# A bidirectional encoder layer on one core: the pool of constants gets another length, so that the tiles above it start elsewhere

## The chip, the cores and the metric

The kernel runs on one core of a Trainium2 chip, in one launch. The metric is the device time of one execution in microseconds (us). The kernel before was run three times; its time is the median of these. The profile is that of one more execution.

## What is computed

One encoder layer (DEPTH is 1) is applied to two groups of tokens with shared weights: 256 tokens of a prompt and 1,024 of a sample, 1,280 rows of 1,024 float32 values in all.

```python
mod = silu(c) @ w_ada + b_ada                       # shift, scale, gate, twice
h = rmsnorm(x, g_pre_mix) * (1 + scale1) + shift1
proj = h @ w_in                                     # 1024 -> 2592 columns
a = rmsnorm(spatial_gating(u_a, v_a, w_s, b_s, g_vn))
o = rmsnorm(gla(q, k, v, g_fwd) + flip(gla(flipped, g_bwd))) * silu(r)
x = x + gate1 * rmsnorm(concat(a, o) @ w_out, g_post_mix)
h = rmsnorm(x, g_pre_ffn) * (1 + scale2) + shift2
up = conv3(h @ w_up) + b_conv                       # 1024 -> 2 * 2816
x = x + gate2 * rmsnorm((silu(gate) * val) @ w_down, g_post_ffn)
```

## The kernel before

**Products.** Nearly every large product is done in three passes: an operand is split into a rounded high part (ACT, L91) and the rest (POOL or DVE, L92), and high x high, low x high and high x low are summed in PSUM. A matmul has a stationary operand (128 columns, loaded as weights) and a moving one (512 columns, or 256 for the prompt alone). TensorE's instructions run in an order written out by hand; so do those of the other engines up to the first 107 us, and from then on a planner orders ACT, DVE, POOL and the DMA queue SP from its own costs.

**Stages**, in the order of time:
- up to 107 us, L347: modulation, transposes of x into the tiles `h1hi` and `h1lo`, and the columns q, k and the gates. The weights are stationary and h1 moves; 240 matmuls of 512 columns, 120 of 256.
- 107 to 457 us, L338 (`group_mm`): four groups of columns of w_in for 10 tiles of tokens, 24 matmuls each, 960 in all, with h1 stationary and weights moving. In between stand the small matmuls of the gated linear attention (L681, L704, L740, L744), of the spatial gating (L573) and `z` (L632, 256 columns).
- 457 to 595 us, L878, L879, L881 (`mix_mm`): the product with w_out, 48 matmuls for each of 10 tiles of tokens, 480 in all. The stationary tiles `mh` and `ml` come from the pool pm for even tiles of tokens and from the pool mixout for odd ones: `prep_m(t + 1, pm if t % 2 else tx)`.
- 595 to 742 us, L1093: the product with w_up for the prompt, 22 blocks of 48 matmuls of 256 columns, with weights stationary and `hp` moving.
- 742 to 1172 us, L1155 (`prod`): the same for the sample by a seven-product scheme, 22 blocks (f) of seven products of 12 matmuls, 1,848 in all; weights are stationary, the prepared `bop` tiles move.
- 1172 us to the end, L1300: the product with w_down, 1,155 matmuls, then the last norm and the output.

**Where tiles lie.** Each of the 128 partitions of the on-chip memory is filled from both ends: pools with `side="right"` are stacked downwards from the top, the others upwards. The first pool on the left is `const` (`cp`); all other pools of the left side start where it ends. In the compiled program it holds these tiles (bytes per partition, in order; a tile takes a multiple of 32):

```
ident 512, mhalf 4 (takes 32), c1 384, cs 1024, sel 256, AB 128, modT1 128,
modT2 128, gc 128, A2 64, B2d 16 (takes 32), c2 704        = 3520
const starts at 16512 and ends at 20032 = 39 x 512 + 64
the right side's first pool (rp, raw tiles) ends at 229344 = 447 x 512 + 480
```

The operand tiles are multiples of 512 bytes long and are cut at multiples of 512 (128 columns of 4 bytes). So every operand of these products on the left starts at remainder 64 of 512, every one on the right at 480. On the left lie `h1` (h1hi, h1lo), `sg`, `sg2`, `mixout` (mh and ml of odd tiles), `hb` (three of the bop_21 tiles), `h2` (hp), `sf` (two weight slots of the sample's up product, S1 to S4, ug, uv, ag, av) and `dn`. On the right lie the weight slots `wp`, `wx`, `wo` and `wr`, `pm` (mh and ml of even tiles), `bo` (all other bop tiles but the five first ones, which use slots of `wp`), the raw tiles and `dr` (both operands of L1300).

In the sample's up product a counter picks the weight slot (L1124):

```python
def wop(name, src, eng=None):
    if wstate["i"] % 8 < 6:
        w = fslot(f"ws{f}_{name}")                                # pool wr, right
    else:
        w = sf.tile([P, 2, 512], F32R, tag="w", ..., bufs=2)      # left
    wstate["i"] += 1
```

It stands at 42 when this stage begins and is raised seven times in each of the 22 blocks, so 38 of the 154 products have their weights on the left. 402 of their 456 matmuls have a moving operand on the right, and 54 one on the left too. Of the other products, 144 matmuls move a bop_21 tile on the left past weights on the right.

**The gates** (`store_gates`, L803). Once, ahead of the group g = 9, DVE forms the 32 columns `gc` in two halves, TensorE transposes them, DVE copies the result into a raw tile `gate_rows`, and SP stores it. Raw tiles come from a pool of four slots:

```python
def raw_tile(name):
    return rp.tile([P, 512], F32, tag="raw", name=name, bufs=4)
```

The loads of w_in, w_out, w_up and w_down pass through the same four slots.

Of the kernel before, what the change touches and what calls it, by code (L numbers as in the profile page):

```python
# [8 lines left out]
F32 = mybir.dt.float32  # L9
# [8 lines left out]
P = 128  # L18
D = 1024
KT = 8  # L20
# [14 lines left out]
def encoder_kernel(ctx: ExitStack, tc: tile.TileContext, x_prompt, x_sample, c_prompt, c_sample,  # L35
# [6 lines left out]
    def pool(name, bufs=1, side="left", space=None):  # L42
        if space is None:
            cm = tc.tile_pool(name=name, bufs=bufs, side=side, reuse_waits="tile")
        else:
            cm = tc.tile_pool(name=name, bufs=bufs, space=space, reuse_waits="tile") if space == PSUM else tc.tile_pool(name=name, bufs=bufs, space=space)
        p = cm.__enter__()
        return p, lambda: cm.__exit__(None, None, None)
# [15 lines left out]
    cp, cp_close = pool("const")  # L64
# [11 lines left out]
    def gtile(name, shape=(P, 512)):  # L76
        gstate.append(gstate.pop(0))
        return gstate[-1].tile(list(shape), F32, tag="g", name=name)
# [8 lines left out]
    def raw_tile(name):  # L87
        return rp.tile([P, 512], F32, tag="raw", name=name, bufs=4)
# [16 lines left out]
    ident = cp.tile([P, P], F32, name="ident")  # L105
    make_identity(nc, ident)
    mhalf = cp.tile([P, 1], F32, name="mhalf")
    nc.vector.memset(mhalf, -0.5)

    su, su_close = pool("startup", side="right")  # L110
# [43 lines left out]
    def col(name, n):  # L154
        return c1[:, R1[name]:R1[name] + n]
# [644 lines left out]
        nc.vector.tensor_copy(wsT, pt)  # L800

    def store_gates():
        gc = cp.tile([P, 4, KT], F32, name="gc")  # L803
        for i, (gate, gname) in enumerate(((mods[1][:, 0:8, :], "g_post_mix"), (mods[2][:, 8:16, :], "g_post_ffn"))):
            nc.vector.tensor_tensor(out=gc[:, 2 * i:2 * i + 2, :], in0=gate.rearrange("p k s -> p s k"),
                                    in1=col(gname, 8).unsqueeze(1).to_broadcast([P, 2, KT]), op=ALU.mult)
        pt = gtile("pt_gate")
        nc.tensor.transpose(pt[0:32, 0:P], gc.rearrange("p s k -> p (s k)"), ident)
        gr = raw_tile("gate_rows")[0:32, 0:P]
        nc.vector.tensor_copy(gr, pt[0:32, 0:P])  # L810
        for i in range(2):
            nc.sync.dma_start(gate_d[i].rearrange("o (r p) -> (o r) p", p=P), gr[16 * i:16 * i + 16, :])

    for g in range(4 * NT):
# [21 lines left out]
        if g == 9:  # L836
            store_gates()
            load_ws()
# [514 lines left out]
```

## Time and profile before

| | us |
|---|---|
| three runs | 1463.11, 1467.68, 1468.05 |
| median | 1467.68 |
| profiled execution, its own time | 1463.15 |
| its span, first to last instruction | 1461.4 |

In the profile PE is TensorE's matmuls, PEld its weight loads, DVE VectorE, ACT ScalarE, POOL GpSimd and SP the queue from which most DMAs are issued. L338 is line 338 of the kernel; a helper's instructions all have the helper's line. A chain row gives a start, a duration, and the engine, tile and line of one merged piece. In a timeline row the first number is a start and the second a busy time, with the last matmul's whole passage through the array; so the spacing of matmuls is read from the starts of two rows and the count (x12) between them, not from the busy time or the mean duration.

### The profile page before, as it was taken

Reading aid. Unit: us, or ns where it says so; the run is one execution under the profiler, and the core shown is the slowest. Engines: PE = TensorE matmul, PEld = TensorE weight load, DVE = VectorE, ACT = ScalarE, POOL = GpSimd, SP = SyncE. Lnnn points to the kernel's source line nnn. Section 1 sums busy time; section 2 is a strip of 40 time slices with the busy share of each in tenths; the row PEclk is TensorE's granted clock in tenths of the full one; section 3 lists DMA queues with packets and bytes.
Section 4 is the critical chain, followed back from the end, with each engine's and each line's share of the span. In section 5 each row is a group of like instructions: output and inputs, shape, how many; then the busy total and the mean of one; then the engine's idle time right before and its main releaser. Section 6 shows DMA issues by size and latency. Waiting matters only on the chain.

```text
span 1461.4 us, 20550 instructions
## 1 busy us (share of the span) xinstructions
PE 1385.5 (95%) x7057; PEld 1131.6 (77%) x7057; DVE 1089.4 (75%) x1653; ACT 692.5 (47%) x1405; POOL 576.3 (39%) x663
## 2 busy tenths in 40 slices
PE   8999989899997999898999999999999989999986
PEld 5886667677776888897978888888888868888875
DVE  5677667877744456798768888788778677879997
ACT  4544465645333234456654555545544345544342
POOL 3356756778763011443454444444444200001011
PEclk9999999999999999999999999999999999999998
DMA  9568542332223442565642222222222288551586
GB/s 300 195 226 289 189 124 84 117 97 63 84 91 110 145 152 101 154 175 156 196 131 85 87 76 66 83 87 87 87 87 80 81 277 307 181 169 65 186 287 207
DMA packets 204107, 210.53 MB, mean 144 GB/s; under 512 B 12968, under 2 KB 157668, under 8 KB 201700
## 3 DMA queue, kind: packets, MB, share of 16 engines
q1 hardware_dynamic: 199976, 200.10, 43.0%
q10 hardware_dynamic: 4028, 9.14, 1.6%
q8 instruction: 55, 0.90, 0.3%
q14 instruction: 48, 0.39, 0.1%
HBM read 171.16 MB, written 38.03 MB: 143 GB/s over the span
## 4 chain that ended last, share of the span: by engine, by line
PE 66%; DVE 10%; issue 7%; DMA 6%; POOL 6%; ACT 4%; SPq 0%; DVEq 0%; POOLq 0%; ACTq 0%
PE upX L1155 16%; PE dn L1300 15%; PE upV L1155 8%; PE ps_gb L338 5%; PE ps_ga L338 4%; PE upY L1155 4%; DMA raw_p<-in_w_up_dram 3%; PE y L878 3%; PE y L879 3%; PE y L881 2%; DVE St L723 1%; POOL macc L466 1%; DVE accP L1041 1%; POOL rstd L98 1%; PE ds L704 1%
## 5 line engine op out<-in xcount | busy, mean ns | idle before, releaser
L1300 PE MATMUL dn<-boM,aoM 128*128 128x512 f32 x1155 | 266.6, 393 | 11.1 <-ACT boM L91 5.9
L1300 PEld LDWEIGHTS dn<-boM,aoM 128*128 128x128 f32 x1155 | 219.4, 190 | 58.2 <-ACT boM L91 6.3
L92 POOL TENSOR_TENSOR ws_S<-S,ws_S 128x512 fp32r<-128x512 f32 x66 | 110.5, 1676 | 102.8 <-ACT ws_S L91 102.8
L1093 PE MATMUL upP<-hp,wp 128*128 128x256 f32 x1056 | 133.7, 287 | 14.4 <-DVE wp L92 12.9
L1093 PEld LDWEIGHTS upP<-hp,wp 128*128 128x128 f32 x1056 | 130.2, 192 | 17.6 <-DVE wp L92 15.4
L1155 PE MATMUL upX<-bop_T,ws_S 128*128 128x512 f32 x528 | 130.0, 395 | 2.8 <-ACT ug L1162 2.8
L92 POOL TENSOR_TENSOR ws<-raw_s,ws 128x512 fp32r<-128x512 f32 x44 | 77.2, 1756 | 120.6 <-ACT ws L91 120.6
L1155 PEld LDWEIGHTS upX<-bop_T,ws_S 128*128 128x128 f32 x528 | 100.0, 189 | 25.8 <-ACT ug L1162 3.3
L338 PE MATMUL ps_ga<-w_a,h1hi 128*128 128x512 f32 x320 | 105.6, 408 | 3.3 <-POOL w_a L92 2.6
L338 PE MATMUL ps_gb<-w_b,h1hi 128*128 128x512 f32 x320 | 105.9, 411 | 1.0 <-DVE w_b L92 0.5
L91 ACT ACTIVATE ws_S<-S 128x512 fp32r<-128x512 f32 x88 | 55.0, 628 | 85.6 <-DVE S L1135 53.8
L92 POOL TENSOR_TENSOR wp<-raw_p,wp 128x512 fp32r<-128x512 f32 x44 | 62.5, 1421 | 75.9 <-ACT wp L91 75.5
L1255 POOL TENSOR_SCALAR fssq<-fssq 128x1 f32<-128x1 f32 x10 | 9.7, 967 | 181.1 <-ACT junk L1252 181.1
L338 PEld LDWEIGHTS ps_ga<-w_a,h1hi 128*128 128x128 f32 x320 | 59.3, 190 | 22.5 <-issue 4.2
L91 ACT ACTIVATE aoM<-saM 128x640 fp32r<-128x640 f32 x55 | 40.6, 740 | 71.7 <-DVE saM L1240 27.4
L1135 DVE TENSOR_TENSOR S<-raw_s,raw_s 128x512 f32<-128x512 f32 x44 | 72.1, 1640 | 3.2 <-DMA raw_s<-in_w_up_dram 3.2
L338 PEld LDWEIGHTS ps_gb<-w_b,h1hi 128*128 128x128 f32 x320 | 57.8, 191 | 14.7 <-issue 2.4
L1041 DVE SCALAR_TENSOR_TENSOR ag<-ug,c,ag 128x1023 f32<-128x1023 f32 x44 | 56.5, 1284 | 15.9 <-ACT ag L1045 15.2
L91 ACT ACTIVATE wp<-raw_p 128x512 fp32r<-128x512 f32 x88 | 53.7, 627 | 30.8 <-DMA raw_p<-in_w_up_dram 25.4
L98 POOL TENSOR_TENSOR rstd<-ms,mhalf 128x2 f32<-128x2 f32 (+1 forms) x90 | 65.3, 726 | 7.3
L338 PE MATMUL ps_gb<-w_b,h1lo 128*128 128x512 f32 x160 | 65.3, 408 | 0.0
L338 PE MATMUL ps_ga<-w_a,h1lo 128*128 128x512 f32 x160 | 65.3, 408 | 0.0
(269 smaller groups left out, 3256.0 us busy)
## 6 DMA issues: line engine op xcount, KB each, us to landing
raw_d<-in_w_down_dram SPq DMA_DIRECT2D x104, 256.0 KB
raw_p<-in_w_up_dram SPq DMA_DIRECT2D x88, 256.0 KB
raw_s<-in_w_up_dram SPq DMA_DIRECT2D x88, 256.0 KB
A<-g_d SPq DMA_DIRECT2D x66, 320.0 KB
wa<-in_w_ada_dram SPq DMA_DIRECT2D x16, 1024.0 KB
g_d<-av SPq DMA_DIRECT2D x22, 512.0 KB
wa<-in_w_ada_dram SPq DMA_DIRECT2D x16, 512.0 KB
vr_d<-vr SPq DMA_DIRECT2D x20, 256.0 KB
```

The source lines that it names most:

```text
L91: nc.scalar.activation(w[:, 0, :], raw, AF.Copy)
L92: (eng or nc.gpsimd).tensor_tensor(out=w[:, 1, :], in0=raw, in1=w[:, 0, :].bitcast(F32), op=ALU.subtract)
L98: nc.gpsimd.tensor_tensor(out=r, in0=ms, in1=mhalf.to_broadcast([P, n]) if n > 1 else mhalf, op=ALU.pow)
L338: nc.tensor.matmul(ps, st, mv, start=(i == 0), stop=(i == n - 1))
L878: nc.tensor.matmul(ys[n], mh[:, kt, :], wos[(kt, n)][:, 0, :], start=(i == 0), stop=False)
L879: nc.tensor.matmul(ys[n], mh[:, kt, :], wos[(kt, n)][:, 1, :], start=False, stop=False)
L881: nc.tensor.matmul(ys[n], ml[:, kt, :], wos[(kt, n)][:, 0, :], start=False, stop=(i == KT - 1))
L1041: nc.vector.scalar_tensor_tensor(out=acc[:, o:o + b - a], in0=src[:, a:b], scalar=c2[:, i, fi:fi + 1], in1=acc[:, o:o + b - a], op0=ALU.mu ...
L1093: nc.tensor.matmul(ps[:, half, :], st, hp[:, hi, kt, :], start=(kt == 0 and i == 0 and half == 0), stop=(kt == KT - 1 and i == 2), skip_gr ...
L1135: nc.vector.tensor_tensor(out=s, in0=a, in1=b, op=op)
L1155: nc.tensor.matmul(ps, w[:, wi, P * j:P * j + P], bops[(b, j)][:, hi, :], start=(start and j == 0 and i == 0), stop=(stop and j == 3 and i ...
L1300: nc.tensor.matmul(pss[j], ao[:, ai, cs_], w[:, wi, :], start=(k == 0 and q == 0), stop=(k == NK - 1 and q == 2))
```

## The change

```diff
     mhalf = cp.tile([P, 1], F32, name="mhalf")
+    cp.tile([P, 8], F32, name="align")
     nc.vector.memset(mhalf, -0.5)
...
     def store_gates():
-        gc = cp.tile([P, 4, KT], F32, name="gc")
+        gc = raw_tile("gc")[:, 0:32].rearrange("p (s k) -> p s k", s=4)
```

A tile of 32 bytes that nothing uses is put into `const`, and `gc` (128 bytes) moves out of it into a raw slot. No instruction is added or taken away. The words that go with the change say that the pool is made 3552 bytes long; by the list above it is 3520 + 32 - 128 = 3424 bytes long and ends at 19936 = 38 x 512 + 480.

## Rows read from the trace of the kernel before

**Rows 1.** The page: busy time by engine; the chain that ended last, by engine.
```profile
PE 1385.5 (95%) x7057; PEld 1131.6 (77%) x7057; DVE 1089.4 (75%) x1653; ACT 692.5 (47%) x1405; POOL 576.3 (39%) x663
...
PE 66%; DVE 10%; issue 7%; DMA 6%; POOL 6%; ACT 4%; SPq 0%; DVEq 0%; POOLq 0%; ACTq 0%
```
**Rows 2.** Timeline of PE, sample's up product, parts of blocks f = 1 to 4.
```profile
783.36 2.97 PE L1155 MATMUL upX<-bop_T,ws 128*128 128x512 f32 x12
786.17 2.91 PE L1155 MATMUL upX<-bop,ws 128*128 128x512 f32 x12
...
799.90 2.88 PE L1155 MATMUL upV<-bop,ws_S 128*128 128x512 f32 x12
802.63 2.97 PE L1155 MATMUL upX<-bop_T,ws 128*128 128x512 f32 x12
...
808.24 2.96 PE L1155 MATMUL upY<-bop,ws 128*128 128x512 f32 x12
811.04 2.92 PE L1155 MATMUL upX<-bop_T,ws_S 128*128 128x512 f32 x12
...
827.49 2.92 PE L1155 MATMUL upY<-bop,ws 128*128 128x512 f32 x12
830.25 2.92 PE L1155 MATMUL upX<-bop_T,ws_S 128*128 128x512 f32 x12
```
**Rows 3.** Timeline of PE, product with w_out, tile t = 1, then t = 2.
```profile
487.91 0.39 PE L878 MATMUL y<-wo,mh 128*128 128x512 f32 x1
...
489.31 0.40 PE L878 MATMUL y<-wo,mh 128*128 128x512 f32 x1
...
494.83 0.39 PE L878 MATMUL y<-wo,mh 128*128 128x512 f32 x1
...
496.19 0.39 PE L878 MATMUL y<-wo,mh 128*128 128x512 f32 x1
```
**Rows 4.** The chain in order of time, pieces of L338 and of L1300.
```profile
236.56 3.29 PE ps_ga L338 x14
...
1179.39 188.51 PE dn L1300 x824
```
**Rows 5.** Timeline of PE: `z` (256 columns) and its follower, and 108 matmuls of L1093.
```profile
230.52 0.28 PE L632 MATMUL z<-L,wg 96*128 96x256 f32 x1
230.64 0.39 PE L338 MATMUL ps_ga<-w_a,h1lo 128*128 128x512 f32 x1
...
711.56 13.25 PE L1093 MATMUL upP<-hp,wp 128*128 128x256 f32 x108 [0.38 <-DVE wp L92]
```
**Rows 6.** The chain by line, of 742:1172, 457:595, 107:457, 0:107, 595:742 us.
```profile
by line: PE upX L1155 55.5%; PE upV L1155 27.6%; PE upY L1155 13.6%; DMA A<-g_d 0.9%; DVE S L1135 0.7%; DVE accP L1041 0.6%; issue 0.4%; ACT accP L1045 0.2%; SPq L1218 0.2%; ACT ws L91 0.1%; ACT ug L1162 0.1%; SPq L1204 0.1%; DVE accP L1102
...
by line: PE y L878 27.0%; PE y L879 26.6%; PE y L881 26.5%; PE pt_m L781 6.5%; PE pt_h L959 5.1%; DMA m<-m_d 3.3%; ACT x L936 0.9%; POOL s L938 0.6%; POOL ua L584 0.5%; POOL rstd L98 0.5%; issue 0.5%; ACT vn L581 0.4%; PE ps_gb L338 0.3%; P
...
by line: PE ps_gb L338 18.8%; PE ps_ga L338 18.0%; issue 6.1%; DVE St L723 5.1%; PE ds L704 3.5%; POOL macc L466 3.1%; PE o L744 2.7%; PE o L740 2.4%; PE sc L681 2.2%; POOL rstd L98 2.2%; POOL gg L640 1.9%; DVE b L642 1.8%; PE mx L573 1.6%;
...
by line: issue 46.4%; PE ps_qkS L347 8.3%; DMA raw_qk<-in_w_in_dram 6.9%; POOL w_a L92 5.2%; POOL macc L466 4.3%; POOL wqk L92 3.6%; POOL rstd L98 3.6%; DMA x<-in_x_sample_dram 3.6%; POOL ms L96 3.3%; PE ps_mod L267 2.8%; ACT h1lo L184 1.9%
...
by line: DMA raw_p<-in_w_up_dram 28.8%; issue 16.3%; DVE accP L1041 8.2%; PE upP L1093 6.7%; ACT wp L91 6.5%; DVE wp L92 4.9%; POOL wp L92 4.5%; ACT accP L1045 4.4%; DVE hs L968 4.0%; DMA raw_s<-in_w_up_dram 3.0%; DVE accP L1102 2.5%; DVE h
```
**Rows 7.** Groups of instructions: DVE making `ml`, and `boM` in L1300's stage.
```profile
L92 DVE TENSOR_TENSOR boM<-sbM,boM 128x512 fp32r<-128x512 f32 x55 | 37.7, 687 | 2.4 <-ACT boM L91 2.3
...
L793 DVE TENSOR_TENSOR ml<-pt_m,mh 128x512 fp32r<-128x512 f32 x20 | 12.9, 684 | 14.0 <-ACT mh L792 14.0
```
**Rows 8.** Writers of `gc` (ns least/median/most, first and last start), and `gate_rows`.
```profile
L805 DVE TENSOR_TENSOR gc<-modT,c x2: 165/712/1260, 142.3 to 169.6; 128x16 f32<-128x16 f32 x2
...
L810 DVE COPY gate_rows<-pt_gate x1: 279/279/279, 173.0 to 173.0; 32x128 f32<-32x128 f32 x1
```
**Rows 9.** The chain in order of time, a load of `raw_a` and its split.
```profile
184.71 3.29 DMA raw_a<-in_w_in_dram
188.02 0.64 ACT w_a L91
```

## The prediction

> **What bounds the kernel now.** Read the page first: TensorE is busy 95% of the span, VectorE 75%, the others half or less, and TensorE holds 66% of the chain of waits that ended last [rows 1]. So a matmul that gets shorter is worth something, but only where it stands on that chain. Next read what each stage's share of the chain is [rows 6]: nearly all of it is matmuls in the sample's up product and in the product with w_out; over a third is L338 between 107 and 457 us, where the small products of the attention and waits for VectorE and GpSimd hold the rest; in the first 107 us and in the prompt's up product (595 to 742 us) it is transfers, splits and "issue". Last read starts in the timeline of TensorE. A busy time there holds a matmul's whole passage; the spacing of starts is what a matmul costs in a stream.
>
> **What a matmul costs, and on what it depends.** The change moves addresses, so the question is whether any row shows the spacing to depend on them. Four pairs of rows in one loop do [rows 2]. Twelve matmuls with weights in a slot of sf (left, remainder 64) and a moving operand on the right (480) take 786.17 - 783.36 = 2.81 us, 234 ns each. Twelve with both on the right take 802.63 - 799.90 = 2.73 us, 227 ns each. Side alone doesn't decide: the Y product of block 4 has weights in sf too, and nine of its twelve matmuls move a bop_21 tile that also lies on the left, so both stand at 64. It takes 830.25 - 827.49 = 2.76 us; less three mixed ones at 234 ns, the nine take 2.06 us, 229 ns each. The Y product of block 3 (weights right, the same nine tiles moving from the left) takes 811.04 - 808.24 = 2.80 us. So it is fast when the two operands' remainders are equal and slow when they differ, in either direction. The product with w_out shows the same with the roles exchanged [rows 3]: tile t = 1 has its stationary operand on the left, and six matmuls take 489.31 - 487.91 = 1.40 us (233 ns); t = 2 has it on the right, and six take 496.19 - 494.83 = 1.36 us (227 ns). L338, all mixed, stands at 3.29 / 14 = 235 ns; L1300, both right, at 188.51 / 824 = 229 ns, whatever held it up included [rows 4]. I take **7 ns for each mixed matmul of 512 columns**; 6 and 7.5 would fit too.
>
> [...]
>
> **What the change does to the addresses.** The pool of constants shrinks from 3520 to 3424 bytes, and every pool above it on the left moves from remainder 64 to 480, that of the right side. All mixed products of the stages above become equal ones; equal pairs stay equal, as both-left ones move together, and the right side is untouched, with L1300 and the attention's own tiles.
>
> **The sum, stage by stage.**
> - L1155: 402 matmuls with weights alone in sf and 144 with a bop_21 tile alone on the left, 546 mixed. This stage's chain is 97% matmuls [rows 6]. 546 x 7 ns = 3.8 us.
> - L878 to L881: odd tiles are mixed, 5 x 48 = 240, and the three lines hold 80% of their stage's chain, all 480 of them [rows 6]. 240 x 7 ns = 1.7 us.
> - L338: all 960 are mixed. On the chain stand 36.8% of 350 us = 129 us, or 550 of them at 234 ns [rows 6]. 550 x 7 ns = 3.9 us. The other 410 run ahead of a wait for VectorE or GpSimd, which then begins earlier and ends at the same time. If all 960 counted it would be 6.7 us; if a shorter product makes half of the 550 wait too, 1.9 us.
> - L347 with 512 columns: 240 mixed, and 8.3% of 107 us on the chain = 38 matmuls [rows 6]. 0.3 us, at most 1.7 us.
> - 256 columns: L1093 (1,056, mixed) and L347 for the prompt (120, mixed). No equal pair of L1093 exists. The nearest row is `z`, both operands on the left: its follower starts 0.12 us later, and L1093's mixed ones take about 13.25 / 108 = 0.12 us too [rows 5]. So I take 0 ns. The other end is the 7 ns of 512 columns, but L1093 holds only 6.7% of its stage's chain, under raw_p's transfers of 28.8% [rows 6]: 0.067 x 147 us / 0.12 us = 82 matmuls, 0.6 us; 1,176 x 7 ns = 8.2 us only if transfers and splits followed.
> - Other engines: VectorE takes 684 ns for `ml`, half of whose tiles lie left and half right, and 687 ns for `boM`, all right [rows 7]. So no gain or loss there. Transfers into the left side also get another remainder; the right side's raw tiles already have it. No row separates the two; I take 0 and leave 1 us either way.
> - `gc` in a raw slot: its two halves and what follows are the same instructions. But its first half ran at 142.3 us, and now the slot that it gets must be free. Until the attention's loads begin the slots hold the gating weights, a modulation row (which `gc`'s second half needs as well) and the first raw_a tiles. So I expect both halves near 169.6 us, where VectorE feeds the attention's start; the least of the two is 165 ns, the most 1,260 ns [rows 8]. I take **0.2 us**, up to 1.3 us. Queued behind it on VectorE are the scans of the attention. SP's loads of raw_a pass through the same four slots; by the last of them (184.71 us) `gc` has been read, before 173.0 us [rows 8, 9], so none waits longer for it. `gate_rows` takes a slot before and after.
>
> 3.8 + 1.7 + 3.9 + 0.3 - 0.2 = **9.5 us**. The profiled execution took 1463.15 us, so one like it would take 1453.7 us. The runs took 1463.11, 1467.68 and 1468.05 us, and their median is 4.5 us above the profiled one. I put the forecast between: the mean of the four times, 1465.5 us, less 9.5 us is **1456 us**, 0.8% below the median. About 0.5% (7.3 us, that is 1460.3 us) is what a measurement of this kernel can tell from no change.
>
> **Rivals.**
> - *Partly eaten.* TensorE in L338's stage waits for the attention's VectorE and GpSimd chain, and the gain of L338 goes there; likewise a few of the others. For it: over 60% of that stage's chain is not L338 [rows 6]. Then 3.8 + 1.7 = 5.5 us are left, less up to 1 us: about 1462 us, within 0.5%. Chance 0.2.
> - *The remainder is not the cause*, or the change doesn't reach it. If the 7 ns came from something else that the left slots of sf, the odd tiles and h1 share, moving them changes nothing; nor would a pool that is really 3552 bytes long (it would end at 20064, remainder 96, still unlike 480). Against it: nine both-left matmuls at 229 ns [rows 2], and the tile list, by which `gc` leaves. Time 1465.5 us, no change. Chance 0.1. [...]
> - *More than the chain shows.* All 1,986 mixed matmuls of 512 columns count, 13.9 us, and some of the 256-column ones: 1465.5 - 13.9 = 1451.6 us, and with half of their 8.2 us 1447.5 us. For it: TensorE is busy nearly throughout [rows 1], and "issue" pieces in the chain of the first 107 us may hide slots that TensorE frees. Chance 0.15.
> - *Slower: the raw ring.* `gc` and `gate_rows` hold two of four slots while the loads of raw_a run, and the planner orders everything after from new times. If loads then go one behind the other, each costs 3.29 us of transfer and 0.64 us of split [rows 9], with SP's loads of q and k queued behind, which start the attention. It decides from three such loads on: 3 x 3.9 = 11.8 us is more than the 9.5 us. With five, the second batch of raw_a, it is 19.7 us and the time 1456 + 19.7 = 1476 us. Against it: `gc` is dead at 173 us, and the last raw_a load comes 11.7 us after. Chance 0.05.
>
> My forecast has 0.5. **Chances:** faster by over 0.5% are the forecast but for some runs on the upper side, and the case of more: 0.62. Within 0.5%: the partly eaten and the unmoved, and the rest of the forecast, 0.32. Slower 0.06. **Range** 1447.5 to 1466.5 us: below the case of more, above the case of no change.
>
> **What the profile would show.** Right: in the timeline the twelve-packs of L1155 that follow weights in sf last 2.73 us like the others; six matmuls of odd tiles in the product with w_out take 1.36 us; 14 of L338 take 3.2 us; L1300 and L1093 stay. The up product of the sample is 3.8 us shorter from end to end, and L338's stage about 4 us. Wrong: spacing stays at 234 ns (the remainder is not it); or it falls to 227 ns and the waits ahead of the attention's products grow as much; or raw_a's loads start later and a wait appears near 190 us.

## The result and the profile after

The kernel with the change takes **1458.44 us** (median of nine runs, 1456.16 to 1461.82) against 1468.05 us before (nine runs, 1462.76 to 1470.83). The ratio is **0.9945, interval 0.9932 to 0.9958**: 8 us of 1467 (6 to 10 us by the interval), just past the half per cent. The two medians lie 9.6 us apart. The profiled execution after took 1459.94 us with a span of 1458.2 us. The order of instructions on every engine is that of before, but for the first half of `gc`, which runs 15 places later on VectorE. New lines are one higher: L338 is now L339, L1155 is L1156.

The page of the kernel after: span, busy times, and the chain that ended last by engine.

```profile
span 1458.2 us, 20550 instructions
...
PE 1378.5 (95%) x7057; PEld 1134.9 (78%) x7057; DVE 1089.3 (75%) x1653; ACT 692.6 (47%) x1405; POOL 576.5 (40%) x663
...
PE 70%; DVE 12%; POOL 5%; DMA 5%; issue 4%; ACT 3%; SPq 0%; DVEq 0%; POOLq 0%; ACTq 0%
```

Against [rows 1] the same 7,057 matmuls keep TensorE busy for 1378.5 us instead of 1385.5 us, and VectorE, ScalarE and GpSimd move by no more than 0.2 us. So the gain is to be looked for in the spacing of matmuls.

Timeline of TensorE after: two starts in the product with w_out (tile t = 1, six matmuls from the one to the other), a long piece of the prompt's up product, and the blocks of the sample's up product from which [rows 2] are taken; start, busy time, line, operands, count.

```profile
490.74 0.39 PE L879 MATMUL y<-wo,mh 128*128 128x512 f32 x1
...
492.10 0.39 PE L879 MATMUL y<-wo,mh 128*128 128x512 f32 x1
...
699.71 12.49 PE L1094 MATMUL upP<-hp,wp 128*128 128x256 f32 x96 [0.18 <-DVE wp L92]
...
783.24 2.88 PE L1156 MATMUL upX<-bop_T,ws 128*128 128x512 f32 x12
785.96 2.88 PE L1156 MATMUL upX<-bop,ws 128*128 128x512 f32 x12
...
799.56 2.88 PE L1156 MATMUL upV<-bop,ws_S 128*128 128x512 f32 x12
802.28 2.88 PE L1156 MATMUL upX<-bop_T,ws 128*128 128x512 f32 x12
805.00 2.88 PE L1156 MATMUL upX<-bop,ws 128*128 128x512 f32 x12
807.72 2.88 PE L1156 MATMUL upY<-bop,ws 128*128 128x512 f32 x12
810.44 2.88 PE L1156 MATMUL upX<-bop_T,ws_S 128*128 128x512 f32 x12
...
826.76 2.88 PE L1156 MATMUL upY<-bop,ws 128*128 128x512 f32 x12
829.48 2.88 PE L1156 MATMUL upX<-bop_T,ws_S 128*128 128x512 f32 x12
```

Every twelve-pack of the sample's up product shown here now takes 2.72 us, 226.7 ns a matmul: the three that took 2.81, 2.80 and 2.76 us in [rows 2] (785.96 - 783.24, 810.44 - 807.72, 829.48 - 826.76) as well as the one that took 2.73 us (802.28 - 799.56). From the Y product of block 3 to that of block 4 there are 826.76 - 807.72 = 19.04 us for 84 matmuls, against 827.49 - 808.24 = 19.25 us in [rows 2]. In the product with w_out the odd tile t = 1 now takes 492.10 - 490.74 = 1.36 us for six, where [rows 3] have 1.40. The 256-column matmuls of the prompt's up product (L1094) are spaced by about 12.49 us / 96 = 0.13 us with what runs into a wait at the end; the mean of their undisturbed spacings is 119.8 ns, and 119.9 ns before.

The chain of waits after, in order of time (start, length, what), and below it the chain by line of 107 to 457 us.

```profile
186.29 3.56 DMA raw_a<-in_w_in_dram
...
189.87 0.64 ACT w_a L91
...
239.95 3.22 PE ps_ga L339 x14
...
1174.60 189.50 PE dn L1301 x824
```

```profile
by line: PE ps_ga L339 15.9%; PE ps_gb L339 15.7%; issue 6.2%; DVE St L724 6.1%; POOL rstd L98 3.1%; PE ds L705 3.0%; DVE St L717 2.4%; DVE b L643 2.4%; POOL gg L641 2.3%; PE o L745 2.2%; DVE b L644 1.9%; DMA wa<-in_w_ada_dram 1.8%; PE o L7
```

Fourteen matmuls of L339 take 3.22 us, 230 ns each, where [rows 4] have 3.29. The `dn` product, whose operands stay where they were, has 189.50 us for 824 against 188.51 in [rows 4]; over ten profiles of both kernels and of variants of either, this piece lies between 188.4 and 189.9 us. The load of `raw_a` and its split stand where [rows 9] have them, 1.6 us later. By line, L339 has 31.6% of this stretch where L338 had 36.8% in [rows 6]. This difference can't be put down to the change: a second profile of the kernel before, unchanged (before_b), has 23.3% there.

```profile
by line: PE ps_gb L338 13.4%; PE ps_ga L338 9.9%; issue 7.0%; DVE St L723 6.4%; POOL gg L640 3.5%; DVE b L642 3.3%; POOL rstd L98 3.3%; POOL macc L466 3.1%; DVE b L643 2.9%; DVE bl L650 2.8%; DVE St L716 2.7%; DVE klp L692 1.7%; ACT bdq L66
```

Over all profiles the share lies between 23.1 and 36.8% in kernels with `h1` where before has it or at another unlike remainder, and between 23.0 and 31.6% where `h1` is aligned. This speaks for several chains of nearly equal length in this stage, of which now one and now another ends last.

The groups of instructions that write `gc`, and its copy (least, median and most ns, first and last start in us):

```profile
L806 DVE TENSOR_TENSOR gc<-modT,c x2: 165/166/167, 169.8 to 171.2; 128x16 f32<-128x16 f32 x2
...
L811 DVE COPY gate_rows<-pt_gate x1: 272/272/272, 174.5 to 174.5; 32x128 f32<-32x128 f32 x1
```

The first half no longer runs at 142.3 us for 1,260 ns [rows 8], but at 169.8 us for some 166 ns, as the step on `gc` expected.

By stage, from the starts of matmuls (us), one execution a row; kernels that have not come up yet follow below. Kernels above the line have `h1` at another remainder than the weights, as before. "To group 4" is the last start of the fourth group of L338 or L339 from the span's start; the stages after it run from the last start of the stage ahead to their own last start. The two up products are added because a stretch with a granted clock of 0.50 instead of 1.00 falls now into the one and now into the other (752.5 to 755.7 us in before, in the sample's; 715.7 to 718.9 us in after, in the prompt's); idle is 350 us less TensorE's busy time from 107 to 457 us.

| kernel | to group 4 | product with w_out | up products | idle |
|---|---|---|---|---|
| before | 457.0 | 134.8 | 579.5 | 20.9 |
| before, again | 456.3 | 136.3 | 579.5 | 21.8 |
| gc_only | 462.4 | 136.1 | 577.8 | 24.0 |
| len3552 | 456.7 | 134.9 | 576.2 | 23.0 |
| h1_back | 459.8 | 133.5 | 573.5 | 22.9 |
| --- | | | | |
| h1_only | 459.5 | 135.3 | 580.5 | 26.4 |
| after | 459.3 | 133.7 | 573.5 | 25.1 |
| after, again | 457.8 | 133.2 | 570.6 | 24.0 |
| align_only | 458.3 | 133.6 | 573.6 | 28.3 |
| base256 | 458.5 | 133.5 | 573.4 | 27.5 |

With the three profiles that hold all operands where before holds them (before, again, gc_only) at 578.9 us and after at 573.5 and 570.6 us, the up products gain 5 us or more, the product with w_out 2 us (135.7 to 133.5). In the time to the end of group 4 no gain can be seen: it lies between 456.3 and 462.4 us above the line, and between 457.8 and 459.5 us below it.

### The profile page after: what moved, and what is told of

Read it like the earlier page. It is cut to its first block, busy times and chain, and to the rows that moved or that the text cites. A ratio compares the mean times of both kernels' runs of the same rounds, so it can differ in the third digit from the quotient of the medians.

```text
span 1458.2 us, 20550 instructions
## 1 busy us (share of the span) xinstructions
PE 1378.5 (95%) x7057; PEld 1134.9 (78%) x7057; DVE 1089.3 (75%) x1653; ACT 692.6 (47%) x1405; POOL 576.5 (40%) x663
## 4 chain that ended last, share of the span: by engine, by line
PE 70%; DVE 12%; POOL 5%; DMA 5%; issue 4%; ACT 3%; SPq 0%; DVEq 0%; POOLq 0%; ACTq 0%
PE upX L1156 16%; PE dn L1301 15%; PE upV L1156 8%; PE upY L1156 4%; PE ps_gb L339 4%; PE ps_ga L339 4%; PE upP L1094 4%; PE ps_qkS L348 3%; PE y L879 3%; PE y L880 3%; PE y L882 2%; DVE St L724 1%; DMA raw_p<-in_w_up_dram 1%; POOL rstd L98 1%; PE ps_qkP L348 1%
## 5 line engine op out<-in xcount | busy, mean ns | idle before, releaser
L92 POOL TENSOR_TENSOR ws_S<-S,ws_S 128x512 fp32r<-128x512 f32 x66 | 113.5, 1723 | 96.7 <-ACT ws_S L91 96.7
L1094 PE MATMUL upP<-hp,wp 128*128 128x256 f32 x1056 | 134.8, 290 | 15.4 <-DVE wp L92 14.0
L1094 PEld LDWEIGHTS upP<-hp,wp 128*128 128x128 f32 x1056 | 131.4, 196 | 18.5 <-DVE wp L92 16.5
L1156 PE MATMUL upX<-bop_T,ws_S 128*128 128x512 f32 x528 | 127.0, 389 | 0.7 <-ACT ug L1163 0.7
L1156 PEld LDWEIGHTS upX<-bop_T,ws_S 128*128 128x128 f32 x528 | 99.1, 188 | 21.6 <-ACT ug L1163 1.1
L339 PE MATMUL ps_ga<-w_a,h1hi 128*128 128x512 f32 x320 | 106.7, 411 | 3.9 <-POOL w_a L92 2.8
L339 PE MATMUL ps_gb<-w_b,h1hi 128*128 128x512 f32 x320 | 105.5, 410 | 1.0 <-DVE w_b L92 0.5
L339 PEld LDWEIGHTS ps_ga<-w_a,h1hi 128*128 128x128 f32 x320 | 60.2, 194 | 23.5 <-issue 5.1
L339 PEld LDWEIGHTS ps_gb<-w_b,h1hi 128*128 128x128 f32 x320 | 58.0, 192 | 14.2 <-issue 2.4
L339 PE MATMUL ps_ga<-w_a,h1lo 128*128 128x512 f32 x160 | 64.9, 405 | 0.0
L879 PE MATMUL y<-wo,mh 128*128 128x512 f32 x160 | 64.6, 404 | 0.0
```

The lines of the kernel that those rows point to most:

```text
L92: (eng or nc.gpsimd).tensor_tensor(out=w[:, 1, :], in0=raw, in1=w[:, 0, :].bitcast(F32), op=ALU.subtract)
L339: nc.tensor.matmul(ps, st, mv, start=(i == 0), stop=(i == n - 1))
L879: nc.tensor.matmul(ys[n], mh[:, kt, :], wos[(kt, n)][:, 0, :], start=(i == 0), stop=False)
L1094: nc.tensor.matmul(ps[:, half, :], st, hp[:, hi, kt, :], start=(kt == 0 and i == 0 and half == 0), stop=(kt == KT - 1 and i == 2), skip_gr ...
L1156: nc.tensor.matmul(ps, w[:, wi, P * j:P * j + P], bops[(b, j)][:, hi, :], start=(start and j == 0 and i == 0), stop=(stop and j == 3 and i ...
```

## Which half of the change does it: gc_only and align_only

The change does two things: it moves `gc` into a raw slot, and it brings the left side to remainder 480. Each alone, against the kernel before.

gc_only keeps the place of `gc` in the pool:

```diff
-        gc = cp.tile([P, 4, KT], F32, name="gc")
+        cp.tile([P, 4, KT], F32, name="room")
+        gc = raw_tile("gc")[:, 0:32].rearrange("p (s k) -> p s k", s=4)
```

> gc takes a raw slot, but its 128 bytes stay reserved in the pool of constants, so that every other tile lies where it lay before (left side at remainder 64). Theory (the remainder is the cause, gc's move is nearly free): mixed matmuls of 512 columns stay at 234 ns, the time stays within 0.3% of before (1463 to 1472 us where before is 1468). Rival (the gain comes with gc's move, for instance over the order of VectorE): about 8 us faster. Second rival (gc's move costs something in the stage of L338, which took 3.0 us more in the profile after): 2 to 4 us slower than before, with the loss between 107 and 457 us.

Measured: 1468.55 us, ratio 0.9999 (0.9985 to 1.0013). Over twelve runs the raw slot costs and gains nothing beyond 2 us either way. The profiled execution of gc_only reaches the end of group 4 some 5 us later than before does (462.4 us in the table), but the runs show no such loss.

align_only leaves `gc` in `const` and moves two other tiles (96 bytes) to the first pool above whose end is then filled up to 512 bytes:

```diff
-    A2 = cp.tile([P, KT, 2], F32, name="A2")
+    A2 = h2p.tile([P, KT, 2], F32, name="A2")
...
-    B2d = cp.tile([P, 4, 1], F32, name="B2d")
+    B2d = h2p.tile([P, 4, 1], F32, name="B2d")
+    h2p.tile([P, 104], F32, name="pad")
```

> gc stays among the constants; A2 and B2d (96 bytes) move to the pool h2, with 416 bytes of padding behind them, so that all left pools start at remainder 480 as in the change. Theory: the whole gain of the change is here, ratio to before 0.993 to 0.996, no matmul of 512 columns spaced at 234 ns, all at 227 ns. Rival (gc's move matters): no gain, 1468 us. If gc's move costs 2 to 4 us in the stage of L338, this kernel is that much faster than the change.

Measured: 1459.2 us, ratio 0.9944 (0.9927 to 0.9961). That is the whole change (0.9945). So the remainder of the addresses is the cause, whichever tiles are moved to reach it.

## Where the gain of L339 went: h1_back and h1_only

The step on L338 expected 3.9 us from `h1` at the same remainder as `w_a` and `w_b`. h1_back takes the kernel with the change and puts only `h1` back to remainder 64; h1_only takes it and puts everything but `h1` back.

```diff
# h1_back: ahead of h1hi
+    h1p.tile([P, 24], F32, name="back")
```

```diff
# h1_only: first tile of the pool hb
+    hb.tile([P, 24], F32, name="back")
```

> The change, but the pool h1 (and sg, sg2 above it) gets 96 bytes of padding, so that h1hi and h1lo lie at remainder 64 again, and mixed matmuls return in L338 and L347 alone (lines of the kernel before); mixout, hb, h2 and sf stay at 480. By the sum of the prediction 4.2 of the 9.5 us are given back: about 1462.5 us, ratio to before 0.996 to 0.998. Rival (the gain of L338 is eaten by the attention's waits): no more than 1 us is given back, ratio as the change's, 0.9945, with the stages from 457 us on alone shorter than before.

> The other half: h1, sg and sg2 lie at 480, and 96 bytes of padding in the pool hb put hb, h2, mixout and sf back to remainder 64. By the sum 4.2 us are gained here, ratio 0.996 to 0.998. Rival (eaten): 0 to 1 us, ratio 0.999 to 1.000, though the matmuls of L338 are spaced at 227 ns.

Measured: h1_back 1459.33 us, ratio 0.995 (0.9932 to 0.9968); h1_only 1466.03 us, ratio 0.9989 (0.9976 to 1.0002). Putting `h1` back costs 0.7 us of the change's gain by the two ratios, less than either interval; having it alone gains 1.6 us, and its interval reaches from no gain to 3.5 us (1 - 0.9976 of 1466). The sum's 3.9 us lies outside.

The matmuls did get shorter: in h1_only L339 is spaced as in the change, 229.0 ns on average where before has 234.0. That is 5 ns and not 7, and not the 227 ns that was expected. By place, the first two spacings behind a small matmul of the attention or a wait average 232 ns (in before 234), the third to eighth 228 to 231, and from the ninth on they stand at 227. So equal matmuls do not reach the short spacing at once here; what holds them back is not shown. TensorE's busy time from 107 to 457 us shows it, first in h1_back, then in h1_only (stretch, its length, TensorE's busy time and matmuls, granted clock, DMA share, GB/s).

```profile
107.00:457.00 350.00, 327.15 (x1728) 0.98 0.39 125
```

```profile
107.00:457.00 350.00, 323.58 (x1726) 0.97 0.40 127
```

3.6 us less busy for the same number of matmuls, and the stretch is as long as before. Over the table, idle in this stretch is 22.5 us on average in the five kernels above the line and 26.3 us in the five below it; none of the first is over 24.0, none of the second under it. Three more kernels with `h1` aligned, scan_a, scan_b and pair below, have 25.1, 24.2 and 26.9 us. The 3.6 us that L339 gives up turn into some 4 us of waiting.

For what? TensorE's waits in the same stretch (engine, line, what it waited for: us in total, times, longest), first h1_back, then h1_only.

```profile
PE mx L575 <- DVE vn L566: 1.5, 2, 1.4
...
PE o L746 <- DVE St L725: 0.6, 1, 0.6
```

```profile
PE mx L574 <- DVE vn L565: 2.5, 2, 2.3
...
PE o L745 <- DVE St L724: 1.3, 2, 1.1
```

Both are results of VectorE that the attention's small products need. With `h1` aligned the wait for `vn` is 2.5, and 1.9 us in the kernel after, and that for `St` 1.3 and 2.1 us. That makes 1 to 2 us of the 4; but `St` alone lies between 0.4 and 3.2 us in the profiles with `h1` aligned, and other rows of the list move both ways by as much between executions. So that the gain becomes idle time is shown. Which wait takes it is shown in part only: it is spread over the list.

## What the remainder has to be: scan_a and scan_b

The `dn` product (L1303 here) is a stream of 1,155 matmuls with both operands on the right, and nothing else depends on where its moving operand lies. Both kernels lengthen the bo tile and cut the operand out of it with another shift in bytes for each of the seven products, on top of the change.

```diff
+SHIFT = (0, 16, 32, 64, 128, 256, 384)      # scan_b: (480, 448, 96, 192, 320, 8, 416)
...
-        wo_ = dr.tile([P, 2, 512], F32R, tag="bo", name=f"bo{name}_{k}", bufs=5)
+        o = SHIFT[i] // 4
+        wo_ = dr.tile([P, 1152], F32R, tag="bo", name=f"bo{name}_{k}", bufs=5)[:, o:o + 1024].rearrange("p (a c) -> p a c", a=2)
```

> On the changed kernel; in the product with w_down the seven products of 165 matmuls each get a moving operand shifted by 0, 16, 32, 64, 128, 256 and 384 bytes against the stationary one's remainder of 512. Theory (only an equal remainder of 512 is fast): the first product is spaced at 227 ns, the six others at 231 to 238 ns. Rival (a smaller unit counts, 64, 128 or 256 bytes): the shifts that are multiples of that unit are at 227 ns, the smaller ones at 231 to 238 ns. [...]

> The same with shifts of 480, 448, 96, 192, 320, 8 and 416 bytes. Theory (only an equal remainder of 512 is fast): all seven at 231 to 238 ns; 96 and 416 bytes are the two distances of the kernel before and stand at 234 ns. Rival (a smaller unit): 192, 320 and 448 are at 227 ns if the unit is 64 bytes, and 96, 416 and 480 too if it is 32 bytes. Second rival: one of them is below 227 ns.

Timeline of TensorE in scan_a, a long piece of each of the products with shift 16, 32, 64, 128 and 256 in this order; below it scan_b, shift 448 and 320.

```profile
1211.72 34.45 PE L1303 MATMUL dn<-boM,aoM 128*128 128x512 f32 x148
...
1249.71 34.46 PE L1303 MATMUL dn<-boM,aoM 128*128 128x512 f32 x147
...
1288.67 34.50 PE L1303 MATMUL dn<-boM,aoM 128*128 128x512 f32 x150
...
1326.69 34.55 PE L1303 MATMUL dn<-boM,aoM 128*128 128x512 f32 x148
...
1364.79 34.41 PE L1303 MATMUL dn<-boM,aoM 128*128 128x512 f32 x151
```

```profile
1216.63 34.70 PE L1303 MATMUL dn<-boM,aoM 128*128 128x512 f32 x148
...
1332.79 34.50 PE L1303 MATMUL dn<-boM,aoM 128*128 128x512 f32 x150
```

A piece less the last matmul's passage (0.39 us), over its count less one, is the spacing. Shift 16: (34.45 - 0.39) / 147 = 231.7 ns; 64: 34.11 / 149 = 228.9 ns; 256: 34.02 / 150 = 226.8 ns; 448: 34.31 / 147 = 233.4 ns. The means over each product, from the starts:

| shift, bytes | 0 | 8 | 16 | 32 | 64 | 96 | 128 | 192 | 256 | 320 | 384 | 416 | 448 | 480 |
|---|---|---|---|---|---|---|---|---|---|---|---|---|---|---|
| ns | 226.8 | 232.2 | 231.7 | 233.3 | 229.0 | 233.3 | 232.3 | 233.3 | 227.0 | 228.9 | 232.6 | 234.2 | 233.3 | 233.3 |

Nothing is below 226.7 ns. A shift of 256 bytes (227.0 ns) costs as little as none (226.8), and 64 and 320, which are 256 apart, give the same value between (229.0 and 228.9). The same holds for 128 and 384 (232.3 and 232.6), and for 192 and 448 (233.3 both). So in these two runs the spacing repeats after 256 bytes and not only after 512. In the kernel before, a moving operand on the right lies 416 bytes beyond weights on the left (480 - 64), the costliest shift of the table (234.2 ns); a moving operand on the left lies at 96 from weights on the right, which costs 233.3 ns.

## The unit in the real kernel: base256 and len3552

Both are the change with another length of the filling tile. base256 leaves the left side at remainder 224, which is 256 from the right's 480. len3552 makes the pool really 3552 bytes long, as the words of the change have it; the left side then starts at remainder 96, 384 from 480.

```diff
-    cp.tile([P, 8], F32, name="align")
+    cp.tile([P, 72], F32, name="align")      # len3552: [P, 40]
```

> The change with a pool of constants of 3680 bytes, so that the left side starts at remainder 224 of 512: 256 bytes from the right side's 480. If 256 bytes are the unit, as the scan of the shifts says (227 ns at 256), all matmuls of 512 columns are at 227 ns and the ratio is the change's, 0.993 to 0.996. If the whole 512 counted, they would be at 234 ns and the ratio 0.999 to 1.001.

> The change with a pool of constants that is really 3552 bytes long: the left side starts at remainder 96, 128 bytes from 480 in units of 256. By the scan (232.3 ns at 128 and at 384) mixed matmuls fall from 234 to 232 ns only, a gain of 2 us at most: ratio 0.998 to 1.001. Rival (the length that the words name is the useful one): ratio 0.9945.

Timeline of TensorE in base256, two products of the sample's up product that begin with weights in sf; below it the same two in len3552.

```profile
801.06 2.88 PE L1156 MATMUL upX<-bop_T,ws 128*128 128x512 f32 x12
803.78 2.88 PE L1156 MATMUL upX<-bop,ws 128*128 128x512 f32 x12
806.50 2.88 PE L1156 MATMUL upY<-bop,ws 128*128 128x512 f32 x12
```

```profile
799.80 2.95 PE L1156 MATMUL upX<-bop_T,ws 128*128 128x512 f32 x12
802.60 2.96 PE L1156 MATMUL upX<-bop,ws 128*128 128x512 f32 x12
805.39 2.95 PE L1156 MATMUL upY<-bop,ws 128*128 128x512 f32 x12
```

base256: 1457.64 us, ratio 0.9937 (0.9916 to 0.9958), packs of 2.72 us. It is the change, without equal remainders of 512. len3552: 1462.48 us, ratio 0.9975 (0.9959 to 0.9991), packs of 2.80 us (802.60 - 799.80), so the mixed ones cost 232.5 to 233 ns and not 226.7. But it gains 3.7 us, where at most 2 us were expected; the interval of the gain, 1.3 to 6.0 us, holds both. Its up products are 3 us shorter than before's; the spacings of L1156 account for 0.7 us of them, and 256-column ones that are spaced at 118.7 ns instead of 119.9 for at most 1.3 us. The rest is not accounted for. What it shows in any case is that a pool of 3552 bytes is not the change: more than half of the gain is missing.

No version measured here is better than the change by more than the intervals; base256 at 0.9937 and the change at 0.9945 overlap almost wholly.

## Which operand meets which: pair

While one matmul runs, the weights of the next are loaded: in the trace after, the weight load of a matmul of L1156 begins 3 ns behind the start of the matmul ahead of it, and takes 188 of the 227 ns. So a slow pair could be a matmul's own two operands, or the operand that streams and the weights that are loaded beside it. In a product by three matmuls (high x high, high weights x low moving, low weights x high moving) the two can be told apart: `pair` shifts only the low half of one operand by 32 bytes, the stationary one in products 1, 3, 5, 7 (set A), the moving one in the others (set B).

```diff
+        e = 8 if i % 2 == 0 else 0
-        ao = dr.tile([P, 2, 640], F32R, tag="ao", name=f"ao{name}_{k}", bufs=4)
+        ao = part(dr.tile([P, 1408], F32R, tag="ao", ..., bufs=4), 640, e)
...
-        wo_ = dr.tile([P, 2, 512], F32R, tag="bo", name=f"bo{name}_{k}", bufs=5)
+        wo_ = part(dr.tile([P, 1152], F32R, tag="bo", ..., bufs=5), 512, 8 - e)
```

(`part` gives the two halves of a tile, the second one moved by that many elements of 4 bytes.)

> On the changed kernel, in the product with w_down only, where three matmuls follow each other: stationary high x moving high (1), stationary high x moving low (2), stationary low x moving high (3). In the first, third, fifth and seventh product the stationary low part is shifted by 32 bytes, so that matmul 3 alone has operands of unlike remainders; in the other three products the moving low part, so that matmul 2 alone has. Theory W (the weights being loaded meet the moving operand that streams just then, which is that of the matmul before): in the first set the start of 2 to the start of 3 is slow (231 to 238 ns), in the second set as well. Theory O (a matmul's own two operands count): in the first set the start of 3 to the start of the next 1 is slow, in the second set that of 2 to 3. In both, what is not slow stands at 227 ns, or a little above it behind a slow one.

Timeline of TensorE in pair, a piece of product 3 (set A):

```profile
1289.59 10.89 PE L1311 MATMUL dn<-boM,aoM 128*128 128x512 f32 x46
```

(10.89 - 0.39) / 45 = 233.3 ns a matmul. By the place in the triple, from one start to the next, means over starts at a granted clock of 1.00, in ns:

| | first to second | second to third | third to first | triple |
|---|---|---|---|---|
| set A, stationary low shifted | 232.4 | 239.3 | 228.1 | 700 |
| set B, moving low shifted | 232.3 | 235.7 | 232.0 | 700 |
| the change, run again | 226.8 | 226.6 | 226.7 | 680 |

In set A the third matmul's own operands differ; by "own operands" its spacing, the last column, would be the long one, and it is the shortest. In set B the second's own differ. The long interval is second to third in both: there the second's moving operand streams while the third's weights are loaded, and these two differ in both sets. This speaks for "the operand that streams against the weights loaded beside it". It does not settle it: one unequal pair of three costs 20 ns a triple, as much as three of them at the same 32 bytes (3 x 233.3 = 700, by the table of shifts), so the price is not paid by the pair alone, and intervals beside it are longer too, where this theory would have 227 ns or a little more. The profiles of before, before_b and gc_only speak both ways. Where a run with both operands on the right meets weights on the left, the last interval of the run stands at 228 ns (17 places in each), which this theory would have at 234. Where a run with both on the left meets weights on the right, it stands at 237 ns (3 places in each), as this theory has it, though the matmul's own two operands are equal there.

## Both kernels once more: before_b and after_b

Both kernels again in one go, unchanged, for a second profile of each.

> The kernel before, profiled once more: the product with w_up for the sample takes 426 to 430 us from its first to its last matmul, the product with w_out 134 to 136 us; TensorE is idle for 20 to 24 us between 107 and 457 us.

> The changed kernel, profiled once more: the product with w_up for the sample takes 421 to 424 us, the product with w_out 133 to 134 us. If L338's gain is eaten by the attention's waits, TensorE is idle for 24 to 28 us between 107 and 457 us and the last matmul of the fourth group starts at 457 to 460 us; if not, idle is 20 to 24 us and that start is at 453 to 456 us.

They took 1465.03 and 1453.81 us, each a single execution. The sample's up product takes 427.9 and 420.8 us from its first to its last matmul: the first as expected, the second 0.2 us under what was expected. The product with w_out takes 136.0 and 133.0 us, at the edge of either range. Timeline of TensorE in before_b, blocks f = 3 and 4 of the sample's up product:

```profile
809.00 2.96 PE L1155 MATMUL upY<-bop,ws 128*128 128x512 f32 x12
811.80 2.92 PE L1155 MATMUL upX<-bop_T,ws_S 128*128 128x512 f32 x12
814.56 2.88 PE L1155 MATMUL upV<-bop_T,ws_S 128*128 128x512 f32 x12
817.28 2.88 PE L1155 MATMUL upX<-bop_T,ws_S 128*128 128x512 f32 x12
820.00 2.88 PE L1155 MATMUL upV<-bop,ws_S 128*128 128x512 f32 x12
822.72 2.88 PE L1155 MATMUL upX<-bop_T,ws 128*128 128x512 f32 x12
825.44 2.97 PE L1155 MATMUL upX<-bop,ws 128*128 128x512 f32 x12
828.25 2.92 PE L1155 MATMUL upY<-bop,ws 128*128 128x512 f32 x12
```

Here a cost can be seen that the sum did not have. The Y product of 809.00 is mixed in nine of twelve and takes 2.80 us. The X product behind it, at 811.80, has both operands on the right, and still takes 814.56 - 811.80 = 2.76 us; only the next ones take 2.72. Slow matmuls have a tail of about 0.04 us here in equal ones behind them. From 809.00 to 828.25 us it is 19.25 us, as in [rows 2]: 84 x 226.7 ns = 19.04, plus 21 mixed ones x 7.4 ns = 0.15, plus 0.06 that is this tail. In after_b there is no tail in this product, and idle in the stretch of the attention is 24.0 us against 21.8 in before_b, with 457.8 and 456.3 us to the end of group 4. Both fall to the case in which L338's gain is eaten, the idle time only just.

## Why the prediction was right, and where its sum was not

The forecast of 1456.0 us lies 2.4 us below the measured median, inside the range, and the likeliest case (faster by over half a per cent) came out, by a little: the gain is 0.55%, and its interval reaches from 0.42 to 0.68%. Its sum of 9.5 us was 8.1 us by the ratio, 9.6 us between the medians. The nearness is partly luck: two terms are off in opposite directions.

- **Price and condition of a mixed matmul.** Right in the sample's up product and in the product with w_out: 7 ns taken; in L1155 mixed matmuls are spaced at 234.1 ns, in L1156 all at 226.7, which is 7.4 ns. L879 to L882 fall from 231.1 to 227.2 ns over odd and even tiles. In L339 the price is smaller, 5 ns (234.0 to 229.0). The first rival, that the remainder is not the cause, is out by align_only against gc_only. In the table of shifts, where only the moving operand's shift differs from product to product, the spacing goes from 226.8 to 234.2 ns.
- **L1155: mis-sized, 3.8 us for 5.** The count was right: the 546 mixed ones hold 4.0 us above 226.7 ns each. What failed is "equal pairs stay equal" in time: they were slower behind mixed ones. Summed over all starts of L1155 (before, before_b and gc_only), the equal ones hold 1.1 us more, 5.1 us in all, and in the kernel after nothing is left of either. The table's 5 us or more for both up products agrees.
- **L878 to L881.** 1.7 us taken; 1.7 us found in the spacings, 2 us in the table.
- **L338: the step that failed.** 3.9 us were taken, with a low end of 1.9; found are 0.7 us (h1_back) to 1.6 us (h1_only), each with an interval that reaches to no gain at all. The term was 550 matmuls on the chain, each paid with 7 ns in full, and all three parts of it were off. The price here is 5 ns. The 550 come from one execution's share of 36.8%; by before_b's 23.3% they would be 350. And what got shorter was not paid: TensorE is busy 3.6 us less between 107 and 457 us and idle 4 us more. That is the prediction's own second sign of being wrong, and in this stage it came true. The rival "partly eaten" described this mechanism correctly, and gave it 5.5 us left and 1462 us (with 1 us lost again and from the forecast's own base, 1465.5 - 5.5 + 1 is 1461 us). The mechanism came, and the size did not, because L1155 had more to give.
- **L347.** 0.3 us taken. Its 512-column matmuls fall from 233.0 to 228.0 ns, but no gain in time can be separated.
- **256 columns.** 0 ns taken, and 119.9 to 119.8 ns found in the change.
- **`gc`: 0.2 us taken;** gc_only's ratio (0.9999, 2 us either way) holds that and nothing at all. The rival of the raw ring is out: `gc` was made at 169.8 us, the order of instructions after it is unchanged, and the load of `raw_a` on the chain takes 3.56 us where [rows 9] have 3.29.
- **The base.** 1465.5 us was taken for before, between its profiled execution and the slower two of its runs; nine runs give 1468.05. The same 9.5 us from there would have been 1458.5 us, against 1458.44 measured.
- **What the premise had wrong.** "Equal remainders of 512" is more than is needed: 256 will do (base256). And the pool is 3424 bytes long; one of 3552 leaves the mixed matmuls at 232.5 ns and gains 3.7 us.

That transfers into the left side gain from their new remainder was left open at 1 us either way. No run separates it.

## What to carry to other kernels

When matmuls of 512 columns stream back to back with new weights each time, read the spacing of starts by pairs of operands: if it comes in two values (here 226.7 and 234.1 ns in L1155), compare the start addresses, and try bringing stationary and moving tiles to the same remainder of 256 bytes with a small filling tile (here 8.1 us by the ratio for the change, 9.2 us for base256, of 1467). Count the gain where a stage is matmuls end to end, and add the equal ones just behind mixed ones (here 1.1 us beside 4.0); where small products wait for other engines, expect the gain to turn into idle time even for matmuls that stand on the chain (here 3.6 us less busy, some 4 us more idle). In such a stage read the chain from more than one profile before a count is taken from it: here the same kernel has 36.8 and 23.3%. A tile added to `const` moves all pools of the left side above it here, so a change of a pool's length can, as in this kernel, bring or take half a per cent (0.55% measured) that has nothing to do with its purpose.

## What had not been expected of the hardware

- In scan_a and scan_b the spacing of 512-column matmuls went by the difference of the two operands' addresses modulo 256 bytes: 227 ns at 0, 229 at 64, 232 at 8, 16 and 128, 233 to 234 at the other multiples of 32 that were tried. That 64 lies between was in none of the theories.
- One unequal pair in three costs as much as three (700 ns a triple for either at a shift of 32 bytes, 680 for none), and an equal run behind a mixed one is slow for some 0.04 us more. What makes it last so long is not shown.
- 256-column matmuls, which take 0.12 us here, show the same spacing with their operands at 64 and 480 as at equal remainders (119.9 and 119.8 ns). In len3552, at 96 and 480, it is a little shorter, 118.7 ns, so equal was not the best for them here.
